# Which engine issues which loads of the scan: merge operands by GpSimd, late weights and attention operands by SyncE

## The chip, the cores and the metric

The kernel runs on one core of a Trainium2 chip. The metric is the device time of one execution in microseconds (us), the median of several runs. The engines are TensorE (PE: matmuls; PEld is its weight load), VectorE (DVE), ScalarE (ACT), GpSimd (POOL) and SyncE (SP), which does nothing but issue transfers (DMAs). Each engine works through its own list of instructions in order. Here DMAs are issued from SP, from ACT and from GpSimd; whichever engine issues one, it waits in its list until what the DMA needs is ready, and what stands behind it in that list waits with it.

## What the kernel computes

One layer of a transformer-like trunk on x of 1024 tokens by 1024 channels, in f32:

```python
mod = silu(c) @ W_ada + b_ada                 # shift, scale and gate, twice
h   = rmsnorm(x) * (1 + scale1) + shift1
proj = h @ w_in                               # q,k,v | delta-net q,k,v,z,beta,decay | branch gates
A = block_attention(rope(q), rope(k), v)      # 8 query heads, 2 kv heads, dim 64
# gated DeltaNet: 8 heads, 16 chunks of 64 tokens, forward and backward
def step(state, inp):
    u_n, w_n, a_n, qg_n, kd_n, gl_n = inp
    v_new = u_n - w_n @ state
    o_n = qg_n @ state + a_n @ v_new
    state = state * gl_n[..., None, None] + jnp.einsum('bhck,bhcv->bhkv', kd_n, v_new)
    return state, o_n
merged = sigmoid(gA) * (A @ W_attn_up) + sigmoid(gB) * (B @ W_dn_up)
x += gate1 * (merged @ W_o)
# then rmsnorm, modulation and a 16-expert SwiGLU MoE in which each expert picks its 128 tokens
```

The scan over chunks is serial: each step needs the state of the one before. `T` in the reference (the inverse of a 64 by 64 lower triangular matrix per chunk and head) is made in the kernel from its two diagonal 32 by 32 blocks' inverses and a merge that fills the block off the diagonal.

## The kernel before, in words

The layer runs as one program of stages: norms and first projections (to about 226 us), the chunk matrices (`dn_tile`, to about 300), their inverses with more projections beside them (to about 364), the **scan** (369 to 716), attention (to about 950), the merge of both branches (to about 1110), and the MoE to the end. The change lies in the scan.

The scan has 16 steps t; step t handles chunk t forward and chunk 15 - t backward. What a step does on PE, by line:

- L654: products of the state with k and q (32 matmuls of 64x64).
- L669: the inverse matrix W times the right side (16). VectorE makes that right side from L654's result (L658, L661).
- L684 and L691: state update and output (16 each; VectorE's L674, L675 ahead of them, L687 and L693 behind them).
- L630 and L637, the **merge** of the chunk matrices for the step after: 16 matmuls of 32x32 each, with ScalarE's L632 and L639 behind them.

Its small matmuls wait for VectorE, so fillers lie between them: the **late projections** (L1209), 14 column groups of 128 of `w_in`, each 48 matmuls of 128x128 by 512 (wh times hTh, wh times hTl, wl times hTh), 672 in all, taken from a generator by `fill(n)` with the counts `FILL = 8, 9, 9, 9, 60` and `END = 6, 6, 6, 6`: 35 in a step, 60 ahead of the first. Each group's weights come with `raw_load` (512 KB, tile wraw with two buffers) one group ahead, and ScalarE (L290, wh) and VectorE (L291, wl) split them into a high and a low part. Also beside the scan run the preparation of attention in steps 0 to 7 (transposes L149, norms and rotary, L744 to L809, whose results are stored to qT_d, kT_d and vS_d), the output of the scan from step 8 on (`scan_post`, L703 to L722), and the late modulation vectors (`mods_late`: loads L919, VectorE's L930 and L932).

A step's operands come through DRAM. `scan_load(t + 2)` issues, at step t, four loads of W (L610), two of the negated inverse blocks n_d (L612, tile name Sc) and two of wt_d (L613): 32 KB each, in runs of 128 bytes, for the **merge**; and further two each of kqs, kv and sa (L618 to L620) for the step itself. n_d and wt_d have one buffer with rows for even and odd chunks, W has two. `attn_load` issues, after step 8, the first operands of attention: two tiles kT (L816, L820), two qT (L818) and vS (L819), together about 3.5 MB.

The program is written for all engines at once; a list scheduler with cost estimates of its own then fixes the order of the instructions on each engine, across stages. So the code's order of `fill` calls isn't the order in which PE runs them, and a change of the issuing engine can change the order on the other engines too.

Of the kernel before, what the change touches and what calls it, by code (L numbers as in the profile page):

```python
# [7 lines left out]
F = mybir.dt.float32  # L8
# [77 lines left out]
class K:  # L86
# [194 lines left out]

    def raw_load(self, col):
        raw = self.wp.tile([128, 8, 128], F, name="wraw", bufs=2)
        self.nc.gpsimd.dma_start(raw, self.i["w_in"][0, :, col:col + 128].rearrange("(k p) c -> p k c", p=128))
        return raw

    def raw_split(self, raw):
# [310 lines left out]
    def scan_load(self, t):  # L598


        nc = self.nc
        w = self.W[t % 2]
        nf, at, kv = self.nf, self.sa[:, t % 2], self.kv[t % 2]
        quads, ns = [], (t, 15 - t)
        kq = [self.kqs[d][:, t % 2] for d in range(2)]
        for d, n in enumerate(ns):
            x = n % 2
            src = self.w_d[d].rearrange("(n h) (b s c) -> n b s h c", h=8, b=2, s=32)
            for b in range(2):
                nc.sync.dma_start(w[64 * x + 32 * b:64 * x + 32 * b + 32, :, b * 32:b * 32 + 32], src[n, b])  # L610
            f, o = slice(64 * x + 32 * d, 64 * x + 32 * d + 32), slice(64 * x + 32 - 32 * d, 64 * x + 64 - 32 * d)
            nc.sync.dma_start(nf[f], self.n_d[d, n].rearrange("h s c -> s h c"))  # L612
            nc.sync.dma_start(self.wt[f], self.wt_d[d].rearrange("(n h) (c s) -> n c h s", h=8, s=32)[n])  # L613
            quads.append((f, o, slice(32 * d, 32 * d + 32), slice(32 - 32 * d, 64 - 32 * d)))
        yield w, at, kv, kq, nf, quads
        for d, n in enumerate(ns):
            r = slice(64 * (n % 2), 64 * (n % 2) + 64)
            nc.sync.dma_start(kq[d], self.kq_d[n])  # L618
            nc.sync.dma_start(kv[r], self.kv_d[n // 2, r])
            nc.sync.dma_start(at[r].rearrange("p h c -> p (h c)"), self.a_d[d, n // 2, r])  # L620
        yield
# [188 lines left out]
    def attn_load(self, bp):  # L810
        nc = self.nc
        self.kT = [bp.tile([128, 2, S], R, name=f"kT{a}") for a in range(2)]
        self.qTs = [bp.tile([128, 512], R, name=f"qT{n}") for n in range(2)]
        self.vS = bp.tile([128, NT, 2, 128], R, name="vS")
        self.rv = self.misc.tile([128, 8, NT], F, name="rv")
        nc.gpsimd.dma_start(self.kT[0].bitcast(F), self.kT_d[0:2].rearrange("h p t -> p h t"))  # L816
        for n in range(2):
            nc.gpsimd.dma_start(self.qTs[n].bitcast(F), self.qT_d[0, :, n * 512:(n + 1) * 512])  # L818
        nc.gpsimd.dma_start(self.vS.bitcast(F), self.vS_d.rearrange("j p (a c) -> p j a c", a=2))  # L819
        nc.gpsimd.dma_start(self.kT[1].bitcast(F), self.kT_d[2:4].rearrange("h p t -> p h t"))  # L820

    def attn_setup(self):
        self.aP = [self.unit(g, (128, 2, 512), R, name="aP") for g in ("g17", "g18", "g12")]
# [863 lines left out]
```

## Time before, and how to read the profile

| | |
|---|---|
| median of three runs | 1728.37 us (1728.33 to 1729.34) |
| the profiled execution | 1728.42 us |
| its span in the trace | 1726.6 us |
| mean granted TensorE clock | 0.967 |
| PE busy | 1616.8 us (94%) |
| DVE busy | 1409.3 us (82%) |
| ACT busy | 907.1 us (53%) |
| POOL busy | 204.3 us (12%) |
| DMA packets, volume | 284146, 388.81 MB |

The profiled execution took 0.05 us more than the median, and 1.8 us lie outside its span. "Clock" or PEclk is the share of full TensorE speed that was granted (1.00 is 2.4 GHz, 0.5 is 1.2 GHz). A window row gives the stretch and its length, then for PE, PEld, DVE, ACT and POOL in this order the busy time and the number of instructions (only PE and PEld where one line alone is asked for), then the mean clock, the share of the 16 DMA engines' time that packets took, and GB/s. A timeline row gives the start, the length, the line and the number of matmuls put together, and in brackets the idle time before it and what ended that.

### The profile page before, as it was taken

The page shows a single profiled execution, that of the slowest core. Times are in us where ns is not written, and L with a number is a line of the kernel's source. Part 1 is how long each engine was busy: PE and PEld are TensorE (multiplying, and loading weights), DVE is VectorE, ACT ScalarE, POOL GpSimd, SP SyncE. Part 2 cuts the span into 40 slices and gives each one's busy share as a digit, 9 for nine tenths or more (in the row PEclk, how much of TensorE's full clock was granted, in tenths as well). Part 3 has the DMA queues.
Part 4 walks back from the last instruction along what each step waited for, and adds up shares of the span by engine and source line. Part 5 has one row for each costly group of instructions (what it writes and reads, how often), then busy time and mean ns, then how long its engine had stood idle before and what let it go on. Part 6 is the DMA issues. An engine that isn't in the chain of part 4 may idle for free. (4 is left out here: it accounts for less than half of the span.)

```text
span 1726.6 us, 30147 instructions
## 1 busy us (share of the span) xinstructions
PE 1616.8 (94%) x11131; PEld 1278.1 (74%) x11131; DVE 1409.3 (82%) x2470; ACT 907.1 (53%) x1352; POOL 204.3 (12%) x196
## 2 busy tenths in 40 slices
PE   6999999889999899699999999669999999999997
PEld 4777778677777677478887788557777777777786
DVE  6899897954667757789986567979999999999996
ACT  6654432122344213288871323347777777777775
POOL 0000022010100100021112312300011000110000
PEclk9999999998999999699999999879999999999999
DMA  9454377257778966721135464769999999999981
GB/s 280 129 175 131 104 181 195 82 179 171 184 197 225 273 176 182 196 86 38 38 111 182 155 209 147 259 227 351 384 379 374 382 388 383 375 377 384 385 309 25
DMA packets 284146, 388.81 MB, mean 225 GB/s; under 512 B 88219, under 2 KB 152399, under 8 KB 283487
## 3 DMA queue, kind: packets, MB, share of 16 engines
q1 hardware_dynamic: 263279, 325.54, 57.4%
q0 software_dynamic: 14096, 48.77, 10.3%
q10 hardware_dynamic: 6624, 12.59, 2.0%
q8 instruction: 88, 1.44, 0.4%
q14 instruction: 59, 0.48, 0.1%
HBM read 328.04 MB, written 58.77 MB: 224 GB/s over the span
## 5 line engine op out<-in xcount | busy, mean ns | idle before, releaser
L1576 DVE TENSOR_TENSOR ew<-er,ew 128x1024 fp32r<-128x1024 f32 x384 | 452.2, 1219 | 29.8 <-ACT ew L1575 29.7
L1575 ACT CAST ew<-er 128x1024 fp32r<-128x1024 f32 x384 | 391.0, 1049 | 137.9 <-PE pj L1629 105.4
L1629 PE MATMUL pj<-ew,xT 128*128 128x512 f32 x1536 | 367.6, 396 | 4.5 <-DVE ew L1576 4.5
L1629 PEld LDWEIGHTS pj<-ew,xT 128*128 128x128 f32 x1536 | 283.2, 188 | 76.2 <-DVE ew L1576 19.5
L1646 PE MATMUL tr<-ew,aT 128*128 128x512 f32 x768 | 191.3, 398 | 0.0
L1646 PEld LDWEIGHTS tr<-ew,aT 128*128 128x128 f32 x768 | 139.7, 188 | 30.4 <-DVE ew L1576 3.4
L297 PE MATMUL pj<-hTh,wl 128*128 128x512 f32 (+1 forms) x384 | 123.4, 399 | 6.5 <-DVE wl L279 6.5
L297 PE MATMUL pj<-hTh,wh 128*128 128x512 f32 (+1 forms) x384 | 122.0, 397 | 3.3 <-ACT hTh L258 1.8
L297 PE MATMUL pj<-hTl,wh 128*128 128x512 f32 (+1 forms) x384 | 121.5, 397 | 1.4 <-DVE hTl L261 1.4
L297 PEld LDWEIGHTS pj<-hTh,wl 128*128 128x128 f32 (+1 forms) x384 | 71.9, 188 | 23.7 <-DVE wl L279 6.9
L297 PEld LDWEIGHTS pj<-hTh,wh 128*128 128x128 f32 (+1 forms) x384 | 70.7, 187 | 20.6 <-ACT hTh L258 1.9
L866 DVE TENSOR_REDUCE am<-pj 128x1 f32<-128x1024 f32 x64 | 77.7, 1216 | 10.0 <-PE pj L861 9.5
L1652 POOL DMA_INDIRECT out_dram<-xe,idxT x16 | 37.2, 2327 | 407.9 <-DVE tok L1550 353.4
L297 PEld LDWEIGHTS pj<-hTl,wh 128*128 128x128 f32 (+1 forms) x384 | 71.2, 187 | 18.6 <-DVE hTl L261 2.0
L1255 PE MATMUL pj<-hTh,uw 128*128 128x512 f32 x256 | 83.5, 404 | 1.0 <-DVE uth L1261 0.5
L868 ACT ACTIVATE ap<-pj,am 128x1024 f32<-128x1024 f32 x64 | 71.8, 1123 | 20.7 <-DVE am L866 11.1
L1209 PE MATMUL pj<-hTh,wh 128*128 128x512 f32 x224 | 79.9, 423 | 0.8 <-ACT y L1214 0.8
L1209 PE MATMUL pj<-hTh,wl 128*128 128x512 f32 x224 | 79.4, 422 | 0.0
L1209 PE MATMUL pj<-hTl,wh 128*128 128x512 f32 x224 | 77.8, 416 | 0.0
L861 PE MATMUL pj<-kT,qT 128*128 128x512 f32 x256 | 76.3, 406 | 0.0
L278 ACT CAST wh<-wraw 128x1024 fp32r<-128x1024 f32 (+1 forms) x26 | 26.7, 1028 | 87.9 <-PE pj L297 87.9
L325 DVE SCALAR_TENSOR_TENSOR y<-xc,colt,y 128x1024 f32<-128x1024 f32 x48 | 61.4, 1279 | 1.4 <-ACT y L323 0.9
(391 smaller groups left out, 2899.0 us busy)
## 6 DMA issues: line engine op xcount, KB each, us to landing
er<-in_w_gate_dram SPq DMA_DIRECT2D x128, 512.0 KB
er<-in_w_up_dram SPq DMA_DIRECT2D x128, 512.0 KB
er<-in_w_down_dram SPq DMA_DIRECT2D x128, 512.0 KB
wraw<-in_w_in_dram POOLq DMA_DIRECT2D x36, 512.0 KB, 5.9
mw<-in_w_ada_dram SPq DMA_DIRECT2D x44, 256.0 KB
wt<-in_w_ada_dram SPq DMA_DIRECT2D x16, 512.0 KB
gate_d<-y ACTq DMA_DIRECT2D x32, 256.0 KB
kqs<-kq_d SPq DMA_DIRECT2D x32, 256.0 KB
```

The lines of the kernel that those rows point to most:

```text
L297: self.nc.tensor.matmul(ps[q][:n], w[:, k, :n], x[k][:, q * 512:(q + 1) * 512], start=(k == 0 and w is wh and x is self.hTh), stop=(k == 7 ...
L325: nc.vector.scalar_tensor_tensor(y, xc[:, t:t + S], w(t), y, op0=OP.mult, op1=OP.add)
L861: nc.tensor.matmul(ps[:, kh], qT[:, i * 128:(i + 1) * 128], self.kT[a][:, s, kh * 512:(kh + 1) * 512], start=(s == 0), stop=(s == 1), skip ...
L866: nc.vector.reduce_max(m, ps, axis=AX.X, negate=True)
L868: nc.scalar.activation(p, ps, AF.Exp, bias=m, scale=1.0, accum_out=self.rv[:, h, half * 4 + i:half * 4 + i + 1])
L1209: nc.tensor.matmul(ps[q], a[:, k], x[k][:, q * 512:(q + 1) * 512], start=(k == 0 and a is wh and x is self.hTh), stop=(k == 7 and a is wl))
L1255: nc.tensor.matmul(ps, w[:, k], v[k][:, qs], start=(k == 0 and p == 0), stop=(k == 3 and p == 2))
L1575: nc.scalar.copy(hi, raw)
L1576: nc.vector.tensor_sub(lo, raw, hi.bitcast(F))
L1629: nc.tensor.matmul(pg[m], x[:, 2 * kp + k], wi[:, k], start=(kp == 0 and k == 0 and n == 0), stop=(kp == 3 and k == 1 and n == 2))
L1646: nc.tensor.matmul(py[q], x[:, k], wi[:, q], start=(k == 0 and n == 0), stop=(k == 7 and n == 2))
L1652: nc.gpsimd.indirect_dma_start(out=out2, out_offset=bass.IndirectOffsetOnAxis(ap=self.idx[:, e:e + 1], axis=0), in_=y, in_offset=None, com ...
```

## The change

The engine that issues two kinds of loads is exchanged. The eight merge loads of each step (L610, L612, L613: 128 in all) go from SyncE to GpSimd. The 13 `raw_load` calls (L284) and the five loads of `attn_load` go from GpSimd to SyncE. No byte, buffer or matmul is added or taken away.

```diff
--- before.py
+++ after.py
@@ -281,7 +281,7 @@
 
     def raw_load(self, col):
         raw = self.wp.tile([128, 8, 128], F, name="wraw", bufs=2)
-        self.nc.gpsimd.dma_start(raw, self.i["w_in"][0, :, col:col + 128].rearrange("(k p) c -> p k c", p=128))
+        self.nc.sync.dma_start(raw, self.i["w_in"][0, :, col:col + 128].rearrange("(k p) c -> p k c", p=128))
         return raw
 
     def raw_split(self, raw):
@@ -607,10 +607,10 @@
             x = n % 2
             src = self.w_d[d].rearrange("(n h) (b s c) -> n b s h c", h=8, b=2, s=32)
             for b in range(2):
-                nc.sync.dma_start(w[64 * x + 32 * b:64 * x + 32 * b + 32, :, b * 32:b * 32 + 32], src[n, b])
+                nc.gpsimd.dma_start(w[64 * x + 32 * b:64 * x + 32 * b + 32, :, b * 32:b * 32 + 32], src[n, b])
             f, o = slice(64 * x + 32 * d, 64 * x + 32 * d + 32), slice(64 * x + 32 - 32 * d, 64 * x + 64 - 32 * d)
-            nc.sync.dma_start(nf[f], self.n_d[d, n].rearrange("h s c -> s h c"))
-            nc.sync.dma_start(self.wt[f], self.wt_d[d].rearrange("(n h) (c s) -> n c h s", h=8, s=32)[n])
+            nc.gpsimd.dma_start(nf[f], self.n_d[d, n].rearrange("h s c -> s h c"))
+            nc.gpsimd.dma_start(self.wt[f], self.wt_d[d].rearrange("(n h) (c s) -> n c h s", h=8, s=32)[n])
             quads.append((f, o, slice(32 * d, 32 * d + 32), slice(32 - 32 * d, 64 - 32 * d)))
         yield w, at, kv, kq, nf, quads
         for d, n in enumerate(ns):
@@ -813,11 +813,11 @@
         self.qTs = [bp.tile([128, 512], R, name=f"qT{n}") for n in range(2)]
         self.vS = bp.tile([128, NT, 2, 128], R, name="vS")
         self.rv = self.misc.tile([128, 8, NT], F, name="rv")
-        nc.gpsimd.dma_start(self.kT[0].bitcast(F), self.kT_d[0:2].rearrange("h p t -> p h t"))
+        nc.sync.dma_start(self.kT[0].bitcast(F), self.kT_d[0:2].rearrange("h p t -> p h t"))
         for n in range(2):
-            nc.gpsimd.dma_start(self.qTs[n].bitcast(F), self.qT_d[0, :, n * 512:(n + 1) * 512])
-        nc.gpsimd.dma_start(self.vS.bitcast(F), self.vS_d.rearrange("j p (a c) -> p j a c", a=2))
-        nc.gpsimd.dma_start(self.kT[1].bitcast(F), self.kT_d[2:4].rearrange("h p t -> p h t"))
+            nc.sync.dma_start(self.qTs[n].bitcast(F), self.qT_d[0, :, n * 512:(n + 1) * 512])
+        nc.sync.dma_start(self.vS.bitcast(F), self.vS_d.rearrange("j p (a c) -> p j a c", a=2))
+        nc.sync.dma_start(self.kT[1].bitcast(F), self.kT_d[2:4].rearrange("h p t -> p h t"))
 
     def attn_setup(self):
         self.aP = [self.unit(g, (128, 2, 512), R, name="aP") for g in ("g17", "g18", "g12")]
```

The scheduler's order moves with it. First GpSimd at the start of the scan: L581 clears the tile W, L284 are loads of late weights, L750 are two products of the rotary table. Before:

```order
L581 MEMSET W 128x1024
L284 DMA wraw<-in_w_in_dram 128x8x128 x2
L750 ISA
L750 TENSOR_TENSOR tab<-rp,rw 128x128 x2
L284 DMA wraw<-in_w_in_dram 128x8x128 x2
L750 TENSOR_TENSOR tab<-rp,rw 128x128 x2
L284 DMA wraw<-in_w_in_dram 128x8x128
L750 TENSOR_TENSOR tab<-rp,rw 128x128 x2
L284 DMA wraw<-in_w_in_dram 128x8x128
```

and with the change:

```order
L581 MEMSET W 128x1024
L612 DMA Sc<-n_d 32x8x32
L610 DMA W<-w_d 32x8x32 x2
L613 DMA Sc<-wt_d 32x8x32
L610 DMA W<-w_d 32x8x32 x2
L612 DMA Sc<-n_d 32x8x32
L613 DMA Sc<-wt_d 32x8x32
L610 DMA W<-w_d 32x8x32 x2
L612 DMA Sc<-n_d 32x8x32
```

GpSimd's list now holds the merge loads in the order of the steps, with nothing else between those of the first steps; its whole list for the scan is these 128 loads and the 16 products L750.

Second, SyncE's list about step 9, where attention's operands stand (L919 are loads of modulation weights, L722 the scan's output going to DRAM, L809 stores of attention's prepared q and k). Before:

```order
L610 DMA W<-w_d 32x8x32
L722 DMA dn_d<-dz 128x4x64 x2
L610 DMA W<-w_d 32x8x32
L612 DMA Sc<-n_d 32x8x32
L613 DMA Sc<-wt_d 32x8x32
L610 DMA W<-w_d 32x8x32 x2
L612 DMA Sc<-n_d 32x8x32
L613 DMA Sc<-wt_d 32x8x32
L919 DMA st<-in_w_ada_dram 128x512
L618 DMA kqs<-kq_d 128x512
```

and with the change:

```order
L809 DMA kT_d<-qst 128x4x128
L816 DMA kT_6104<-kT_d 128x2x1024
L722 DMA dn_d<-dz 128x4x64 x2
L818 DMA qT_6106<-qT_d 128x512
L818 DMA qT_6107<-qT_d 128x512
L819 DMA vS<-vS_d 128x8x256
L820 DMA kT_6105<-kT_d 128x2x1024
L618 DMA kqs<-kq_d 128x512
L619 DMA kv<-kv_d 64x1024
L620 DMA sa<-a_d 64x512
```

The merge loads are gone from SyncE's list, and the five loads of `attn_load` (L816 to L820) stand in it, right ahead of the kqs, kv and sa loads of a later step; the 13 loads of L284 stand at other places of the same list, two of them ahead of the first kqs load.

Third, PE in the last two steps of the scan (L861 are score matmuls of attention, L945 a product of the modulation vectors, L149 transposes). Before:

```order
L861 MATMUL pj<-kT_6104,qT_6107 128x512 x8
L669 MATMUL dn<-st,W 64x64 x16
L684 MATMUL dn<-st,kv 64x64 x8
L691 MATMUL dn<-st,sa 64x64 x16
L630 MATMUL tr<-Sc 32x32 x16
L684 MATMUL tr<-st,kv 64x64 x8
L654 MATMUL dn<-Sc,kqs 64x64
L637 MATMUL tr<-W,pt 32x32 x16
L654 MATMUL dn<-Sc,kqs 64x64 x31
L945 MATMUL tr<-macc,ones 1x512
L669 MATMUL dn<-st,W 64x64 x13
```

and with the change, in the last step:

```order
L669 MATMUL dn<-st,W 64x64 x16
L1209 MATMUL pj<-hTl_571,wh 128x512 x2
L1209 MATMUL pj<-hTh_570,wl 128x512 x2
L1209 MATMUL pj<-hTh_611,wh 128x512 x2
L691 MATMUL dn<-st,sa 64x64 x16
L1209 MATMUL pj<-hTl_612,wh 128x512 x2
L1209 MATMUL pj<-hTh_611,wl 128x512 x2
L1209 MATMUL pj<-hTh_652,wh 128x512 x2
```

Before, all 672 fillers stand ahead of the first of these rows: they have run out in step 13, no L1209 stands between the matmuls of the last two steps, and those steps have eight score matmuls. In the middle of the scan from 35 to 46 fillers stand between one step and the next. With the change 35 stand in every step, as a rule 18 of them ahead of L654, 8 between L654 and L669 and 9 between L669 and L684; L630 stands right ahead of L669, and L637 behind L691. Some 64 fillers are left behind the last step, with the first 16 score matmuls among them (32 stood ahead of the end of the scan before). On VectorE 16 of the 40 instructions of L930 and L932 now stand in steps 2 to 6; before, all 40 stood from step 8 on.

## Rows read from the trace of the kernel before

**Rows 1.** The page's part 2: the span in 40 slices of 43 us.

```profile
PE   6999999889999899699999999669999999999997
PEclk9999999998999999699999999879999999999999
```

**Rows 2.** Windows: stretches inside the scan, all engines.

```profile
382.20:401.15 18.95, 13.38 (x148) 9.15 (x146) 1.07 (x2) 2.07 (x5) 1.75 (x3) 0.64 0.89 176
401.15:554.00 152.85, 148.93 (x2229) 115.90 (x2225) 105.14 (x281) 60.30 (x135) 12.43 (x21) 1.00 0.73 194
685.00:715.80 30.80, 19.40 (x372) 14.87 (x370) 25.16 (x52) 6.85 (x13) 0.00 (x0) 0.72 0.67 172
369.00:715.80 346.80, 316.48 (x4441) 241.48 (x4440) 225.02 (x548) 104.60 (x218) 20.30 (x32) 0.94 0.76 201
```

**Rows 3.** Windows, the filler line L1209 alone.

```profile
382.20:401.15 18.95, 9.33 (x20) 5.27 (x18) 0.64 0.89 176
369.00:715.80 346.80, 189.91 (x672) 124.35 (x672) 0.94 0.76 201
499.79:517.18 17.39, 10.17 (x35) 6.18 (x35) 1.00 0.68 174
617.99:641.48 23.49, 17.18 (x66) 11.58 (x65) 1.00 0.67 171
```

**Rows 4.** Windows: two whole periods of the scan, all engines.

```profile
499.79:517.18 17.39, 17.31 (x258) 13.06 (x250) 11.22 (x32) 6.24 (x15) 0.88 (x2) 1.00 0.68 174
617.99:641.48 23.49, 23.49 (x292) 17.19 (x292) 15.67 (x34) 6.38 (x11) 0.00 (x0) 1.00 0.67 171
```

**Rows 5.** Timeline of PE: start, length, line, count, idle before.

```profile
387.12 0.28 PE L630 MATMUL tr<-Sc 32*32 32x32 f32 x2 [4.32 <-DMA Sc<-wt_d]
...
428.07 0.62 PE L1209 MATMUL pj<-hTh,wh 128*128 128x512 f32 x2
...
435.33 0.62 PE L1209 MATMUL pj<-hTl,wh 128*128 128x512 f32 x2
...
448.09 0.63 PE L149 MATMUL tr<-masks,hl 128*128 128x128 f32 x4 [0.95 <-DVE hl L795]
...
605.90 0.28 PE L630 MATMUL tr<-Sc 32*32 32x32 f32 x2 [7.45 <-DMA Sc<-wt_d]
...
606.71 1.05 PE L1209 MATMUL pj<-hTh,wh 128*128 128x512 f32 x2
...
611.83 0.57 PE L1209 MATMUL pj<-hTh,wh 128*128 128x512 f32 x1
```

**Rows 6.** Waits from 366 to 720: total, times, longest.

```profile
PE tr L630 <- DMA Sc<-wt_d: 14.5, 4, 7.5
```

**Rows 7.** Waits of SP's DMA queue, 366 to 720.

```profile
SPq L768 <- DVE vst L767: 38.6, 8, 14.4
```

**Rows 8.** Timeline of SP's queue, 585 to 606.

```profile
591.01 0.93 SPq L722 DMA_DIRECT2D dn_d<-dz  x2
...
592.53 4.40 SPq L612 DMA_DIRECT2D Sc<-n_d  x1
```

**Rows 9.** Groups of GpSimd (POOL) instructions, 200 to 720.

```profile
L525 POOL DMA_DIRECT2D n_d<-nn x32 | 18.6, 584 | 42.6 <-DVE nn L518 40.0 <-DVE e L510 2.3 <-issue 0.3
L284 POOL DMA_DIRECT2D wraw<-in_w_in_dram x13 | 11.7, 897 | 181.4 <-DVE wl L291 81.3 <-DVE ro_a L121 28.1 <-DVE wl L279 21.5
```

**Rows 10.** Source view of L284: issue to landing.

```profile
DMA to landing us min/median/max: 4.4/6.7/8.2
```

**Rows 11.** Source view of L525: issue to landing.

```profile
DMA to landing us min/median/max: 1.9/2.9/5.7
```

**Rows 12.** Source view of L612 on SP: one issue, ns.

```profile
L612 SPq DMA_DIRECT2D Sc<-n_d x32: 302/428/4399, 378.4 to 695.4; - x32
```

**Rows 13.** Groups of VectorE (DVE) instructions, 369 to 716.

```profile
L658 DVE TENSOR_TENSOR st<-dn,egs 128x256 f32<-128x256 f32 x64 | 24.3, 417 | 27.8 <-PE dn L654 27.7
L930 DVE SCALAR_TENSOR_TENSOR macc<-mw,cs,macc 128x512 f32<-128x512 f32 x14 | 10.4, 744 | 0.7 <-DMA mw<-in_w_ada_dram 0.7
```

## The prediction, made before the changed kernel ran

> **What bounds the kernel now.** The page comes first: PE has a 9 in most slices of 43 us; within the scan (slices 9 to 17) the busy digit falls to 8 in slices 9 and 14 and to 6 in 17, and the clock's to 8 in 10 and to 6 in 17 [rows 1]. Slices hide what is shorter, so the scan was then cut into windows. In its middle, from 401 to 554, PE is busy 148.93 of 152.85 us at clock 1.00, 97.4%: there PE itself is the limit, and DVE with 105.14 us isn't. The whole scan, 369 to 715.8, has PE busy 316.48 of 346.80 us at a mean clock of 0.94 [rows 2]. So the scan loses time in a few places, not everywhere. The timeline and the waits of PE tell which:
>
> 1. The start, 382.2 to 401.15: clock 0.64, PE busy 13.38 of 18.95 us [rows 2]. The first merge stands still for 4.32 us for wt [rows 5].
> 2. Step 11's merge at 598: PE stands 7.45 us for wt, and the 13 fillers after it run at half speed [rows 5]. All waits of PE for wt are 14.5 us in four [rows 6]. SyncE was late: its L722 store went out only at 591.0, L612 behind it took 4.40 us to issue [rows 8], against a median of 0.43 [rows 12].
> 3. The end, 685 to 715.8: no fillers are left (PE's order above), 372 small matmuls keep PE busy only 19.40 of 30.80 us at clock 0.72 [rows 2], each waiting for DVE, which is busy 25.16 there.
>
> **What is lost there, worked out.** A filler at full clock costs (435.33 - 428.07) / 32 = 0.227 us [rows 5]. A small matmul costs, from one period without idle time (17.39 us, 258 matmuls, 35 of them fillers [rows 3, 4]), (17.39 - 35 x 0.227) / 223 = 0.042 us.
>
> - Start: 20 fillers [rows 3] and 128 others are 4.5 + 5.4 = 9.9 us of work in 18.95: 9.0 lost.
> - Step 11: 7.45 of idling, and 14 fillers at 0.43 instead of 0.227 (606.12 to 612.33 is 13 of them after 606.71 [rows 5]): 3.0. Together 10.5.
> - End: 364 x 0.042 + 8 scores x 0.227 = 17.1 us of work in 30.8: 13.7 lost.
>
> Sum 33.2 us. A check by another way: the scan's busy time at its mean clock is 316.48 x 0.94 = 297.5 us of full-speed work; at the middle's 97.4% that takes 305.4, so 41.4 of the 346.8 us could go. With no idle time at all it would be 49.3, the most that can be won here. I take the middle of the two ways, 37.
>
> **The change part by part.**
>
> *Merge loads off SyncE.* 128 issues at a median of 0.428 us [rows 12] are 55 us of SyncE's list. None of it is on PE's path by itself; what counts is that a merge load no longer stands behind L722 or L768, whose waits on SyncE run to 14.4 us [rows 7]. This is what removes place 2's wait and most of place 1's.
>
> *Merge loads on GpSimd.* The trace of before has no such load there. The nearest rows are n_d's stores, the same 32x8x32 shape from the same engine: 584 ns each [rows 9], landing after 2.9 us, at most 5.7 [rows 11]; the upper bound is L284's 897 ns [rows 9] and its 8.2 us [rows 10]. Eight a step are 4.7 us (up to 7.2) of a 17.4 us period, with about 0.9 us of rotary products: GpSimd isn't full either way. I take 584, the same shape. A set is wanted two steps after its buffers come free, some 35 us, so 5.7 or 8.2 us of landing is covered. If that cover goes, the price is the landing time, per step: 16 x 2.9 = 46 us; I see nothing that takes it away, since GpSimd's list holds nothing else that waits.
>
> *The order on PE.* This is the bigger half. With every step holding 35 fillers, the last two steps aren't bare any more (place 3), and the 64 fillers and 16 scores behind the last step hide its sums. The fillers don't cost anything new: 672 stay 672 [rows 3]. Steps 11 to 13 had up to 66 fillers in one period (23.49 us [rows 3, 4]); by the same unit costs that period with 35 is 23.49 - 31 x 0.227 = 16.5 us. The 16 scores that move behind the scan cost the attention what they cost here: nothing net.
>
> *Late weights and attention operands on SyncE.* 18 issues, 13 of 512 KB. They cost SyncE some 18 x 0.43 = 8 us, far under the 55 it gives up. What they do is wait: L284 waits until VectorE has split an earlier group (GpSimd waited 81.3 us for it, which cost nothing there [rows 9]). On SyncE kqs, kv, sa, attention's stores and the L919 loads stand behind. kqs, kv and sa are double-buffered and issued a step ahead, 17 us; a wait of a few us is covered, one like L768's 14.4 [rows 7] isn't quite.
>
> *VectorE.* 16 L930 and L932 in steps 2 to 6 are 16 x 0.744 = 11.9 us [rows 13], 2.4 a step on top of 105.14 / 152.85 x 17.4 = 12.0: 14.4 of 17.4. And the new order leaves less between L654 and L669: 8 fillers and 16 L630 are 1.8 + 0.7 = 2.5 us, while VectorE needs three L658 (1.25 [rows 13]) and one subtraction of twice their size, about 0.8 as an estimate, 2.1 in all. If it is later than that by 0.4 us, PE waits. Such just-in-time waits are there now too, 0.95 us for hl [rows 5]. I charge 1 us in each of five full steps, 5 us; between 0 and 15 (every step) are the bounds.
>
> **Sum.** 37 - 5 = 32 us off. The profiled execution, 1728.42 us, stands 0.05 from the median, so no correction: **1696 us**. A difference under 0.2% (3.5 us) is about what a measurement here can't tell from none.
>
> **Rivals.**
>
> *Just-in-time waits in every step.* For it: the spacing 18, 8, 9 is tight, and DVE's list is long. Against: the middle of the scan runs at 97.4% with DVE at 69% [rows 2]. About 15 steps x 1 us instead of 5: 1706, with lower clock after the waits up to 1711; I put it at 1708.
>
> *The burst stalls again, on another load.* attention's 3.5 MB now stand in SyncE's own list right ahead of kqs, kv and sa. For it: beside that burst an issue took 4.40 us [rows 8]. Against: kqs has a step of lead. If PE stands as long as it did in step 11, 10.5 us come back: 1707.
>
> *The transfers were hidden anyway.* Only the four waits for wt, 14.5 us [rows 6], go, and the end of the scan stays as long because VectorE bounds it (25.16 of 30.80 us [rows 2]): 1714. The Trainium skill, "DMA: Bandwidth & Descriptors", section "Issuing engines are not separate DMA queues", says that DMAs of all engines end on the same 16 DMA engines, and that issuing from several saves only the sequencer's time, usually small; by that rule alone SyncE's 55 us, off PE's path, would bring nothing. Here the trace speaks against it: the stall of step 11 went with an issue of 4.40 us and the wait ahead of it, which are the sequencer's [rows 8].
>
> *No change.* What is won in the scan is waited for in attention, whose first operands arrive no sooner; the page shows clock and busy digits at 9 right behind the scan [rows 1], so this is unlikely: 1728.
>
> *Slower: late weights.* L284 stands in SyncE's list behind stores that wait, L768 for up to 14.4 us [rows 7], and lands 6.7 us after its issue [rows 10]. A group's matmuls can't start without it, and the small matmuls of the scan stand behind them in PE's list. Eleven groups load inside the scan, so each us of lateness costs up to 11; it decides from (32 + 3.5) / 11 = 3.2 us late each. With the landing wholly exposed, 11 x 6.7 = 74 - 32: 1770. Against: a load has one whole group, 48 fillers or some 24 us, of lead.
>
> **How the numbers follow.** My forecast, with its own range 1686 to 1703: 0.54. Waits in every step: 0.14. The burst again: 0.13. Hidden anyway: 0.06. No change: 0.05. Slower: 0.08. The range reaches up over the three partial cases to 1716 and down to what is left if the second way holds nearly whole (41 of 49 us without the charge for VectorE, and some of place 1's start earlier): 1678. What lies outside is no change, slower, and a few in a hundred below. Faster is the first four, 0.87; same 0.05; slower 0.08.
>
> **What would show it.** In the changed kernel's trace: L630 and L637 wait for no DMA (place 1 and 2 right); the clock is 1.00 from about 390 to the end of the scan; periods of 16.5 to 18 us in all 16 steps; a scan that ends some 32 us sooner, with the same length behind it. Wrong would be: waits of L669 or L684 for VectorE of over 1 us in most steps (first rival); a wait of L654 for kqs at about step 11 (second); the last steps as long as before (third); L1209 waiting for wl or wh, and SyncE's list waiting before L284 (the slower one). Steps 2 to 6 are where I expect the worst periods.

## The result, and the profile after

The changed kernel takes 1708.97 us (median of 4 runs, 1706.11 to 1711.86) against 1728.72 us in the runs of before beside it (1728.33 to 1729.34). The ratio is 0.9885, with a 95% interval of 0.9867 to 0.9904: 19.8 us faster, 1.15%. The forecast was 1696, 32 us. The time lies in the range of 1678 to 1716, but outside the forecast's own 1686 to 1703; the profiled execution, 1710.1 us, has a span of 1708.3.

First the page, its slices now 42.7 us long; rows of before are [rows 1]:

```profile
PE   5999999897979989999999999579999999999997
PEclk9999999998989999999999999789999999999999
```

The notch at the end of the scan, a 6 in both lines in slice 17, is gone: 16 and 17 have a 9. Now slices 10 and 12 have a 7 for PE and an 8 for the clock. The windows say the same (columns as in [rows 2]):

```profile
382.20:401.15 18.95, 9.93 (x144) 8.10 (x145) 3.89 (x9) 3.67 (x10) 2.52 (x5) 0.69 0.96 188
401.15:554.00 152.85, 137.64 (x2290) 110.94 (x2293) 118.47 (x310) 60.25 (x134) 56.50 (x89) 0.94 0.91 241
685.00:715.80 30.80, 28.38 (x134) 20.73 (x132) 16.69 (x20) 18.33 (x33) 8.83 (x7) 1.00 0.53 168
369.00:715.80 346.80, 307.36 (x4494) 240.41 (x4492) 239.50 (x578) 112.66 (x235) 96.04 (x150) 0.93 0.82 219
```

The end, 685 to 715.8, went from 19.40 us of PE time at clock 0.72 to 28.38 at 1.00. The start, 382.20 to 401.15, won nothing: 9.93 us of PE time now, 13.38 before [rows 2]. And the middle, which had been PE's own limit with 148.93 us busy at 1.00, is down to 137.64 at 0.94. So the change took out the bare end, left the start, and opened new places in the middle.

The last L691 of the scan starts at 679.1 instead of 714.0, but 64 fillers and all score matmuls lie behind it now; the first L1255 of the merge stage starts at 873.5 instead of 891.7, 18.2 earlier, and from there on all is shifted by 18 to 19 us. The whole difference arises in the scan and in the first us of attention.

Step by step the new middle looks like this. Each row is one period, from the start of L654 to the next one's, steps 1 to 7:

```profile
413.00:432.60 19.60, 17.04 (x280) 13.90 (x279) 14.67 (x38) 7.63 (x19) 8.16 (x12) 0.91 0.97 236
432.60:450.25 17.65, 16.16 (x278) 12.95 (x277) 12.77 (x33) 7.08 (x17) 4.62 (x8) 1.00 1.04 290
450.25:469.00 18.75, 16.23 (x278) 12.99 (x277) 12.77 (x37) 7.62 (x17) 6.02 (x10) 1.00 0.83 222
469.00:491.40 22.40, 18.07 (x278) 14.61 (x277) 19.48 (x51) 7.43 (x17) 8.68 (x11) 0.85 0.88 222
491.40:514.20 22.80, 18.58 (x278) 14.96 (x277) 18.02 (x43) 9.09 (x21) 7.89 (x12) 0.85 0.89 248
514.20:530.00 15.80, 15.70 (x278) 12.81 (x277) 13.21 (x36) 7.39 (x16) 6.03 (x10) 1.00 1.03 288
530.00:545.70 15.70, 15.70 (x278) 12.81 (x277) 13.48 (x36) 7.62 (x18) 4.63 (x8) 1.00 0.77 197
```

The last two rows are a step with nothing in its way: PE is busy 15.70 of 15.80 and of 15.70 us, with the same 278 matmuls. The prediction's unit costs gave 16.5 to 17.4. Of the 15.7 us the 243 matmuls that aren't fillers take 15.7 - 35 x 0.227 = 7.8; before, in the period from 460.48 to 479.64, PE was busy 18.77 us with 287 matmuls, 43 of them fillers, so that the 244 others took 18.77 - 43 x 0.227 = 9.0. The new order has them in longer runs, with fewer changes between small and large matmuls; that this is why was not tested. The five rows ahead of the last two are 2 to 7 us longer, 22.7 us in sum, and DVE is busy up to 19.48 of 22.40 us there. Behind step 7 two more periods are long, those of steps 10 and 13:

```profile
577.70:596.84 19.14, 16.48 (x261) 12.84 (x260) 13.57 (x31) 4.14 (x8) 4.61 (x8) 0.82 0.95 232
628.76:650.35 21.59, 17.56 (x267) 12.61 (x266) 16.88 (x44) 4.24 (x8) 2.30 (x4) 0.84 0.72 192
```

What PE waits for, at the start and in step 4, by its timeline:

```profile
385.27 0.66 PE L630 MATMUL tr<-Sc 32*32 32x32 f32 x30 [3.10 <-DMA Sc<-wt_d]
...
392.45 1.69 PE L654 MATMUL dn<-Sc,kqs 64*64 64x64 f32 x62 [2.58 <-DMA kqs<-kq_d]
...
397.50 1.51 PE L149 MATMUL tr<-masks,qraw 128*128 128x128 f32 x6 [3.37 <-DMA qraw<-qkv_d]
...
476.56 1.09 PE L149 MATMUL tr<-masks,hl 128*128 128x128 f32 x4 [4.33 <-DVE hl L795]
```

The start waits for wt, then kqs, then qraw; step 4 waits 4.33 us for hl, VectorE's last product of the preparation. That wait costs more than itself: the period is 22.40 us instead of 15.70, PE is busy 18.07 us of it for the 15.70 us of work, and the clock from 476.5 to 482.5 is 0.57. Of the other long periods step 1 waits 2.56 us for qraw, a DMA, step 10 stands 2.54 us at L669 for nothing that the profile names, and step 13 waits 4.03 us for the scan's own output on VectorE (L714), which makes PE's largest sum of waits from 366 to 720:

```profile
PE tr L149 <- DVE st L714: 9.0, 6, 4.0
```

VectorE in turn waits for the loads of the modulation work. Its largest wait from 405 to 520:

```profile
DVE macc L930 <- DMA mw<-in_w_ada_dram: 7.2, 3, 3.1
```

With the other tiles of these loads (mb, st and L932's mw) that is 13.4 us. The merge itself is out of the way: PE's waits for wt, 14.5 us in four before [rows 6], are one of 3.1, at the start, where GpSimd's load itself stands 3.6 us until the stage before has stored wt_d. GpSimd's groups from 360 to 700:

```profile
L610 POOL DMA_DIRECT2D W<-w_d x64 | 36.9, 583 | 32.4 <-PE dn L669 27.9 <-DMA w_d<-wb 3.2 <-issue 1.2
L612 POOL DMA_DIRECT2D Sc<-n_d x32 | 18.8, 588 | 95.6 <-PE tr L630 88.7 <-PE dn L669 4.5 <-DMA Sc<-n_d 2.3
L613 POOL DMA_DIRECT2D Sc<-wt_d x32 | 18.6, 582 | 7.0 <-DMA wt_d<-wtmp 3.6 <-DMA Sc<-wt_d 3.1 <-issue 0.2
```

and the source view of L612:

```profile
DMA to landing us min/median/max: 2.3/5.3/10.5
```

128 issues at 582 to 588 ns, where the prediction took 584 from n_d's stores [rows 9]. GpSimd spends its time waiting for PE to free the buffers (88.7 us before L612), so the loads go out as early as they can, some two steps ahead. They land after a median of 5.3 us, at most 10.5, more than the 2.9 and 5.7 taken from the stores [rows 11], and behind the start it doesn't matter, since they have two steps.

### The profile page after: what moved, and what is told of

It reads as the page before. It is cut to its first block, busy times and chain, and to the rows that moved or that the text cites. A ratio compares the mean times of both kernels' runs of the same rounds, so it can differ in the third digit from the quotient of the medians.

```text
span 1708.3 us, 30169 instructions
## 1 busy us (share of the span) xinstructions
PE 1593.8 (93%) x11131; PEld 1267.3 (74%) x11131; DVE 1409.8 (83%) x2470; ACT 906.1 (53%) x1352; POOL 274.8 (16%) x306
## 3 DMA queue, kind: packets, MB, share of 16 engines
q10 hardware_dynamic: 6624, 12.59, 2.0%
## 5 line engine op out<-in xcount | busy, mean ns | idle before, releaser
L866 DVE TENSOR_REDUCE am<-pj 128x1 f32<-128x1024 f32 x64 | 77.9, 1217 | 19.5 <-PE pj L861 19.0
L1255 PE MATMUL pj<-hTh,uw 128*128 128x512 f32 x256 | 83.4, 403 | 1.0 <-DVE uth L1261 0.5
L1209 PE MATMUL pj<-hTh,wh 128*128 128x512 f32 x224 | 77.6, 423 | 0.0
L1209 PE MATMUL pj<-hTh,wl 128*128 128x512 f32 x224 | 77.5, 418 | 0.0
L861 PE MATMUL pj<-kT,qT 128*128 128x512 f32 x256 | 74.7, 403 | 2.2 <-ACT ap L868 1.9
L1209 PE MATMUL pj<-hTl,wh 128*128 128x512 f32 x224 | 75.5, 413 | 0.0
```

What stands on the lines that cost most here:

```text
L861: nc.tensor.matmul(ps[:, kh], qT[:, i * 128:(i + 1) * 128], self.kT[a][:, s, kh * 512:(kh + 1) * 512], start=(s == 0), stop=(s == 1), skip ...
L866: nc.vector.reduce_max(m, ps, axis=AX.X, negate=True)
L1209: nc.tensor.matmul(ps[q], a[:, k], x[k][:, q * 512:(q + 1) * 512], start=(k == 0 and a is wh and x is self.hTh), stop=(k == 7 and a is wl))
L1255: nc.tensor.matmul(ps, w[:, k], v[k][:, qs], start=(k == 0 and p == 0), stop=(k == 3 and p == 2))
```

## The experiments

Theory 1: the gain is the even spread of fillers plus merge loads that no longer stand behind SyncE's waits; what is missing is PE waiting for VectorE in steps 1 to 5. Theory 2: late weights have to leave GpSimd for the merge loads to have a free list. Theory 3: what is missing is the transfer engines at the start and a half clock behind any wait. Each run is compared with the kernel before on the same chip (medians 1729.0 to 1730.6 there).

**Halves of the change.** The first run moves the merge loads alone.

```diff
-                nc.sync.dma_start(w[64 * x + 32 * b:64 * x + 32 * b + 32, :, b * 32:b * 32 + 32], src[n, b])
+                nc.gpsimd.dma_start(w[64 * x + 32 * b:64 * x + 32 * b + 32, :, b * 32:b * 32 + 32], src[n, b])
...
-            nc.sync.dma_start(nf[f], self.n_d[d, n].rearrange("h s c -> s h c"))
+            nc.gpsimd.dma_start(nf[f], self.n_d[d, n].rearrange("h s c -> s h c"))
...
```

> Half of the change alone: the 128 merge loads on GpSimd, the late weights and attention's operands stay on GpSimd as before, so all stand in one list. The order on PE is that of the changed kernel (35 fillers in every step). Theory 1 (the gain comes from the even spread of fillers and from merge loads that are no longer behind SyncE's stores; the missing part is PE waiting for VectorE): about 1709 us, within 1704 to 1714. Theory 2 (the late weights have to leave GpSimd, because a merge load behind an L284 that waits for VectorE stalls PE): waits of L630 for DMA come back, 1716 to 1730.

1706.6 us, ratio 0.9879 (0.9854 to 0.9904): the whole gain. Theory 2 falls. The second run moves the other half alone, L284 and `attn_load` to SyncE:

```diff
-        self.nc.gpsimd.dma_start(raw, self.i["w_in"][0, :, col:col + 128].rearrange("(k p) c -> p k c", p=128))
+        self.nc.sync.dma_start(raw, self.i["w_in"][0, :, col:col + 128].rearrange("(k p) c -> p k c", p=128))
...
-        nc.gpsimd.dma_start(self.kT[0].bitcast(F), self.kT_d[0:2].rearrange("h p t -> p h t"))
+        nc.sync.dma_start(self.kT[0].bitcast(F), self.kT_d[0:2].rearrange("h p t -> p h t"))
...
```

> The other half alone: late weights and attention's operands on SyncE, merge loads on SyncE as before, so GpSimd has neither. Here fillers reach to the last step too (39, 34, 35, 38, 23, 40 and so on, 551 ahead of the last L654, before 612 of 612). Theory 1, if the spread of fillers is the larger part: the bare end goes, some 14 us, the waits for wt stay: 1712 to 1718. Rival (the gain is the merge loads' own queue): nothing is won and SyncE's list is longer by 18 loads: 1728 or above.

1760.0 us, ratio 1.0184 (1.0157 to 1.0212): 31 us slower, against theory 1, and more than a list longer by 18 issues explains. This is the prediction's slower rival, late weights, come true in another kernel. SyncE's queue in this run:

```profile
587.20 0.38 SPq L816 DMA_DIRECT2D kT<-kT_d  x1
593.44 0.93 SPq L722 DMA_DIRECT2D dn_d<-dz  x2
594.42 1.00 SPq L818 DMA_DIRECT2D qT<-qT_d  x2
595.58 0.37 SPq L819 DMA_DIRECT2D vS<-vS_d  x1
596.00 0.58 SPq L820 DMA_DIRECT2D kT<-kT_d  x1
...
597.46 0.66 SPq L284 DMA_DIRECT2D wraw<-in_w_in_dram  x1
```

its timeline of PE:

```profile
610.05 1.22 PE L1209 MATMUL pj<-hTh,wh 128*128 128x512 f32 x2 [11.33 <-ACT wh L290]
```

and its waits from 366 to 760:

```profile
ACT wh L290 <- DMA wraw<-in_w_in_dram: 27.7, 7, 8.8
...
PE pj L1209 <- ACT wh L290: 23.7, 5, 11.3
```

SyncE issues kT, then stands till 593.44 for VectorE's dz; behind that come the rest of attention's operands and only then a raw load, at 597.46. ScalarE waits for it before it can make wh, and PE stands 11.33 us. In all ScalarE waits 27.7 us for wraw and PE 23.7 for wh; in the changed kernel ScalarE's wait is 3.8 us in one. So the second half does harm while SyncE's list is full, and none when the 128 merge loads are gone from it.

The third run of this group is the changed kernel with attention's five loads back on GpSimd (the last diff's lower part undone).

> The changed kernel with attention's five operand loads back on GpSimd: merge loads and those five on GpSimd, late weights on SyncE. If the burst of 3 MB in SyncE's list ahead of kqs, kv and sa costs something (a rival of the prediction), 3 to 8 us faster, 1701 to 1706; if not, 1707 to 1711.

1709.0 us, ratio 0.9897 (0.9874 to 0.992): no difference. Which engine issues that burst doesn't show in the time. It shows in the trace: on GpSimd merge loads behind the burst stand 4.1 and 3.7 us until its vS and kT have landed, and PE's stall at L669 in step 10 is 7.3 us instead of 2.5.

**Half of the merge loads.** The next two runs leave all else as it was before and move either L610 or L612 and L613. In both the order on PE is the even one.

```diff
-                nc.sync.dma_start(w[64 * x + 32 * b:64 * x + 32 * b + 32, :, b * 32:b * 32 + 32], src[n, b])
+                nc.gpsimd.dma_start(w[64 * x + 32 * b:64 * x + 32 * b + 32, :, b * 32:b * 32 + 32], src[n, b])
```

> Only the 64 loads of W (L610) go to GpSimd; the n_d and wt_d loads (L612, L613), for which PE waited before, stay on SyncE, as do all others where they were. The order on PE is the even one (35 fillers a step, 531 ahead of the last L654), and VectorE's modulation work stands from step 7 on. Theory 1a (the even order carries the gain): 1695 to 1706. Theory 1b (the wait for wt behind SyncE's list has to go): L630 still waits for DMA, 1712 to 1725.

```diff
-            nc.sync.dma_start(nf[f], self.n_d[d, n].rearrange("h s c -> s h c"))
-            nc.sync.dma_start(self.wt[f], self.wt_d[d].rearrange("(n h) (c s) -> n c h s", h=8, s=32)[n])
+            nc.gpsimd.dma_start(nf[f], self.n_d[d, n].rearrange("h s c -> s h c"))
+            nc.gpsimd.dma_start(self.wt[f], self.wt_d[d].rearrange("(n h) (c s) -> n c h s", h=8, s=32)[n])
```

> Only the 64 loads of n_d and wt_d (L612, L613) go to GpSimd, W stays on SyncE. The order on PE is the even one here too, modulation work from step 6 on. Theories 1a and 1b both: 1693 to 1705. If it needs all 128 off SyncE: 1712 to 1725, with waits of L637 for W.

1712.0 us, ratio 0.9905 (0.988 to 0.993), and 1715.1, ratio 0.9919 (0.9907 to 0.9932). The waits from 366 to 720 with W alone moved (its profiled execution, span 1721.0, was one of its longer ones):

```profile
PE tr L630 <- DMA Sc<-wt_d: 8.6, 2, 5.5
PE tr L149 <- DMA qraw<-qkv_d: 8.6, 5, 5.8
```

and with n_d and wt_d alone:

```profile
PE dn L669 <- issue: 14.8, 2, 11.0
PE dn L654 <- DMA kqs<-kq_d: 8.3, 2, 5.3
...
PE tr L149 <- DMA qraw<-qkv_d: 5.7, 4, 4.0
```

With wt left on SyncE PE still waits 8.6 us for it. With wt on GpSimd it waits 3.6 for wt, but kqs (8.3) and qraw are late, which have always been SyncE's, and not W, as was expected. PE also stands 14.8 us at L669 there for nothing that the profile names, the longer time (11.0) from 587.0 on, when SyncE had just taken 10.87 us to issue four loads of W (574.59 to 585.46); whether W is what it waits for isn't shown. Theory 1a, that the even order carries the gain, fails with both runs: it wanted 1706 or less. Theory 1b, that the wait for wt has to go, was too narrow: in these two runs wt, kqs and qraw, left in the longer SyncE list, are late. In both runs the modulation work stands from step 6 or 7 on, so they are to be compared with the next pair, not with the changed kernel.

**VectorE in steps 2 to 6.** The changed kernel with one tiny instruction, through which the late modulation work depends on step 7:

```diff
+                cs = self.misc.tile([128, 8], F, name="csl")
+                self.nc.vector.scalar_tensor_tensor(cs, self.X[:, 0, 0:8], 0.0, self.cs, op0=OP.mult, op1=OP.add)
+                self.cs = cs
                 behind.append(self.mods_late(MODG, 8))
```

> The changed kernel, with the late modulation work (L919 loads beyond the first four, L930, L932) made to depend on step 7 by a small VectorE instruction, so that it can't stand in steps 2 to 6. Theory 1 (VectorE's added work and its waits for L919 in steps 2 to 6 make PE wait for hl and the state): the long periods of 19 to 23 us shrink, 1701 to 1705. Theory 3 (the missing part is DMA contention at the start and the half clock behind any wait): 1707 to 1711, as the changed kernel.

1695.9 us, ratio 0.9806 (0.9781 to 0.9831): 13.1 below the run with attention's loads back, which is the changed kernel's time on that chip. The middle, in the same window as above:

```profile
401.15:554.00 152.85, 145.53 (x2479) 117.36 (x2477) 126.28 (x335) 63.43 (x140) 58.65 (x90) 0.97 0.94 253
```

and two of its periods, steps 4 and 5:

```profile
464.65:480.54 15.89, 15.89 (x278) 12.80 (x278) 13.37 (x37) 7.22 (x18) 6.04 (x10) 1.00 1.00 256
480.54:496.21 15.67, 15.67 (x279) 12.74 (x278) 13.37 (x36) 7.49 (x17) 6.96 (x10) 1.00 0.99 272
```

2479 matmuls instead of 2290 in the same 152.85 us, and steps 2 to 6 take 15.67 to 15.94 us, without a wait of VectorE for these loads: theory 1's cause, with more behind it than was expected of it. Step 1, with its wait for qraw, stays at 20.03 us, and the held work is paid for later in part: step 8 takes 21.57 us there. The same edit on the kernel that moves the merge loads alone:

> Merge loads on GpSimd, late weights and attention's operands left on GpSimd, and the late modulation work held to step 7 as in the earlier run of that kind. If the exchange of the late weights does nothing for the gain and the held work gives its 13 us here too: 1690 to 1700. If late weights in the merge loads' own list cost something once VectorE isn't the limit: 1702 to 1708.

1698.2 us, ratio 0.9816 (0.9803 to 0.9828). Both halves of the change together are worth no more than the first here either. Against these two the halves of the merge loads are 14 to 19 us slower: about as much as the even order with half of the loads had brought. So the even order alone isn't the gain; taking the rest of the merge loads off SyncE is worth as much again.

**Another list.** The merge loads on ScalarE's list, all else as before (`nc.scalar` for `nc.gpsimd` in the first diff):

> As the run with the merge loads alone moved, but to ScalarE's list in place of GpSimd's. The order on PE is the even one, modulation work stands in steps 1 to 4. If all that counts is that they leave SyncE's list: 1702 to 1712, as there. If the list they stand in has to be free of waiting work: a load behind a waiting L762 or L290 stands, and ScalarE's own work stands behind a load that waits, 1715 to 1740.

1717.3 us, ratio 0.9921 (0.9902 to 0.9941), in the second of the two ranges, at its lower end. Waits from 366 to 720, of ScalarE and of PE:

```profile
ACT qst L807 <- DMA W<-w_d: 19.0, 3, 7.7
PE tr L630 <- DMA Sc<-wt_d: 8.9, 3, 4.2
```

L807, a product of attention's preparation, needs no W, so it stood behind a load in ScalarE's list that waited. Leaving SyncE's list, with the even order, brings 13 us even so; the list of an engine with waiting work of its own costs some 7 (by the ratios) to 11 us (by the medians) of the 22 again. The two intervals touch, so the size is rough.

**The start and the burst.** On the held kernel the rotary weights' six small loads (L732, L736) go ahead of the inversion stage, their tile in another pool:

```diff
-        self.rw = self.misc.tile([128, 2, 2, 64], F, name="rw")
+        self.rw = self.ab.tile([128, 2, 2, 64], F, name="rw")
...
+            self.rope_weights()
             with ExitStack() as st2:
...
             self.scan_setup()
-            self.rope_weights()
```

> The changed kernel with the held modulation work, and the six small loads of the rotary weights (L732, L736) issued before the inversion stage, so that SyncE's list goes straight on to kqs, kv, sa and qraw at the start of the scan. If the start is lost because these stand behind nine us of issues: the waits for kqs and qraw (some 9 us in the profile) shrink, 1688 to 1693. If the transfer engines are full there whatever the order: 1693 to 1699, as with the hold alone.

1683.7 us, ratio 0.9734 (0.9721 to 0.9748): 12.2 below the held kernel, more than was expected. SyncE's queue at the start in the changed kernel:

```profile
367.94 0.33 SPq L732 DMA_DIRECT2D rw<-in_q_norm_w_dram  x1
368.33 4.76 SPq L736 DMA_DIRECT2D rw<-in_q_norm_w_dram  x2
...
377.08 0.41 SPq L618 DMA_DIRECT2D kqs<-kq_d  x1
```

the same in this run:

```profile
368.16 2.71 SPq L618 DMA_DIRECT2D kqs<-kq_d  x1
```

the stretch between, first in the changed kernel and then in this run:

```profile
377.00:382.20 5.20, 5.17 (x25) 3.93 (x23) 1.68 (x3) 1.54 (x2) 2.06 (x5) 1.00 0.33 87
377.00:382.20 5.20, 5.20 (x24) 4.32 (x23) 0.00 (x0) 0.68 (x1) 3.32 (x6) 1.00 1.08 282
```

and this run's window of the start:

```profile
382.20:401.15 18.95, 15.55 (x311) 12.31 (x310) 11.77 (x33) 5.29 (x14) 8.90 (x15) 1.00 1.09 250
```

In the changed kernel kqs goes out at 377.08, behind 9 us in which SyncE issues six loads of 16 and 32 KB; here at 368.16, and PE is busy 15.55 of the 18.95 us at clock 1.00 instead of 9.93 at 0.69. So the transfer engines (theory 3) weren't what bound the start: in the changed kernel their share is 0.33 from 377.0 to 382.2, while kqs has only just gone out, and here it is 1.08 there and 1.09 behind it. PE's first wait for wt shrinks too, from 3.78 us in the held kernel to 1.22, and step 1, which had waited for qraw, is down from 20.0 to 16.2 us.

Attention's five loads, spread over steps 8 to 11, each made to wait for its step by a tiny copy into its tile:

```diff
+        x = self.X[:, 0, 0:8]
+
+        def mark(t):
+            nc.vector.tensor_copy(t, x)
+
+        yield
+        mark(self.kT[0][:, 0, 0:8])
         nc.sync.dma_start(self.kT[0].bitcast(F), self.kT_d[0:2].rearrange("h p t -> p h t"))
+        yield
...
```

> The changed kernel with the held modulation work, and attention's five operand loads spread over steps 8 to 11, each behind a tiny VectorE copy that depends on its step. If the stall near step 10 (4.3 us inside L669 in the profile of the held run, and the half clock behind it) comes from the burst of 3 MB: 1689 to 1693. If it has another cause: 1694 to 1699.

1689.3 us, ratio 0.9778 (0.976 to 0.9795): 6.6 below the held kernel, but that one ran on another chip and the two intervals overlap, so this pair doesn't show a gain. And both:

> Both edits on the held kernel. If both places are worth what their waits show: 1682 to 1689. If neither: 1694 to 1699.

1676.4 us, ratio 0.9698 (0.9685 to 0.9711), 53 us below the kernel before and the fastest here, faster than was expected of both. On the same chip it is 7.3 us below the run with the early rotary weights alone and 12.9 below the one with the spread alone, with intervals apart: that is what each edit is worth on top of the other. Its page's part 2:

```profile
PE   6999999899998999999999999399999999999997
PEclk9999999999999999999999999699999999999999
```

and its windows of the start and the scan:

```profile
382.20:401.15 18.95, 17.77 (x342) 14.23 (x345) 13.43 (x37) 7.30 (x18) 7.39 (x14) 1.00 1.12 266
...
369.00:715.80 346.80, 327.94 (x4687) 258.88 (x4686) 269.28 (x623) 142.01 (x288) 96.67 (x150) 0.99 0.83 221
```

From slice 2 to 17 PE stands at 8 or 9, and the clock at 9 throughout the scan.

**The control:** all three edits on the kernel before, with no engine exchanged.

> The control: the kernel before, no engine exchanged, with all three edits of the fastest run (rotary weights early, attention's operands spread over steps 8 to 11, modulation work held to step 7, where it stood anyway). The order on PE is the uneven one, the last two steps bare. If these edits work without the exchange, the start and step 11 come out, 53 of the fastest run's us less some 15 for the bare end: 1690 to 1700. If the merge loads in SyncE's list and the bare end are what binds first: 1712 to 1728.

1722.4 us, ratio 0.9952 (0.9938 to 0.9965). 8 us, where they bring 33 on top of the exchange. Its window of the end:

```profile
685.00:715.80 30.80, 18.76 (x266) 12.45 (x261) 23.83 (x57) 6.32 (x12) 0.00 (x0) 0.62 0.79 211
```

PE's waits for wt are down from 14.5 to 1.3 us without any exchange, and kqs goes out at 380.29 instead of 385.88, still behind merge loads; the last L691 starts at 704.4 instead of 714.0. But the order stays uneven and the end as bare as before (19.40 us at 0.72 [rows 2]). So the waits for wt of places 1 and 2, taken away by themselves, are worth 8 us, where the prediction charged 19.5 for these places; at the start PE is then busy 14.25 us of the 18.95, at 0.91.

## Why the prediction was right in part

*The places.* Place 3, the bare end, was right: the window of the end went from 0.72 to 1.00. That the order is its cause, not the end's own work, is shown by the runs: in both with half of the loads moved, which have the even order, PE is busy 29.2 and 29.4 of its 30.8 us at 1.00; in the control, with the uneven order but hardly a wait for wt, 18.76 at 0.62. How much of the 19.8 us it carries isn't shown: no run has the even order with all merge loads on SyncE. Place 2, step 11's wait for wt, went as foreseen. Place 1, the start, 9.0 us of the sum, was not won at all, and this is a step that failed: it took the wait for wt [rows 5] behind SyncE's stores to be the cause, but on GpSimd PE still waited 3.1 us for wt, and then for kqs and qraw, which stood behind the rotary weights' issues in SyncE's list. The early rotary weights brought 12 to 13 us, part of them in step 1, so this term was about right in size and wrong in what would release it.

*GpSimd.* 584 ns an issue, taken from the stores, was 582 to 588; that two steps of lead cover the landing held, though the landing was twice what was taken.

*VectorE.* This is the term that was mis-sized: 5 us charged for steps 2 to 6, 13.1 measured by taking the cause away. The prediction had the place, the cause (16 more instructions there) and the bounds (0 to 15), and took the lower third. Two things were missing. VectorE waits in order for the L919 loads that come with that work, 13.4 us from 405 to 520; and behind a wait of some us PE ran at the lower clock (0.57 from 476.5 to 482.5), so that step 4's wait of 4.33 us made its period 6.7 us longer. The held run moves work and loads together, so how much of the 13 us is VectorE's time and how much its waits for L919 stays open.

*The sum.* 37 less 9 for the start and 13 for VectorE is 15; 19.8 were measured. What the working left out goes both ways, and no run closes the account. A clean step takes 15.7 us, not 16.5; and the first us of attention, where PE had stood for VectorE three times between 715.8 and 720 (0.97, 1.40 and 1.09 us), are now filled but for 0.60. Against that the periods of steps 10 and 13 are 3.4 and 5.9 us longer than a clean one. The check by another way took PE's busy time for work; the same small matmuls took 9.0 us of it in the old order and 7.8 in the new, so that the limit given, 49.3 us, wasn't one: the fastest run won 53. A small slip: 14 fillers at 0.43 instead of 0.227 us are 2.8 us, not 3.0.

*The rivals.* Just-in-time waits came nearest: 1706 to 1711 was given for them, 1709 measured, but by luck, since the waits are few and long and are those of L149 for hl and for the scan's output, not of L669 or L684 in most steps. The burst, spread out, gives 7.3 us, less than the 10.5 given; that was run with the burst on SyncE only. That the transfers were hidden anyway is refuted by the gain at the end and by the run with the merge loads alone: what counted is what 128 issues and their waits stand ahead of, and the order that came with moving them. The Trainium skill's rule ("DMA: Bandwidth & Descriptors", "Issuing engines are not separate DMA queues") is that another issuing engine saves only sequencer time, usually little. The 22 us of the run with the merge loads alone don't refute it, because the order on PE and VectorE changed along with the issuer. Late weights, the slower rival, didn't come in this kernel, and came with 31 us in the one where SyncE kept the merge loads: the mechanism was right, and it came only where the merge loads were still in that list.

*The marks.* L630 and L637 waiting for no DMA: nearly (one wait of 3.1 us). The clock at 1.00 from 390: wrong, 0.94. Periods of 16.5 to 18 us: 15.7 where nothing waits, up to 22.8 in steps 2 to 6, which were named as the worst, and 21.6 in step 13, which wasn't named.

## What to carry to other kernels

Put loads that a serial stage needs just in time in a list where little else waits, and ask what else stands there: GpSimd's list brought 22 us (and fewer packets, below), ScalarE's, with waiting work of its own, 13. The exchange's second half (moving other loads the other way) may be worth nothing, as here, or 31 us of loss if the first is missing. Under a scheduler with costs of its own, read the new order on all engines before costing a change of one queue: here an exchange of DMA engines spread the fillers evenly (a part of the gain) and pulled foreign work onto VectorE and the transfer engines (13 us of loss), and one tiny instruction that adds a dependence gave it back. When one wait is taken away, list what else arrives in the same us: at the start kqs and qraw stood right behind wt.

## What the runs showed of the hardware

*Packets.* The same 128 merge loads, 4.2 MB, are cut differently by the issuing engine. GpSimd's queue on the pages of the kernel before and of the run that moves the merge loads alone (packets, MB, share of the 16 engines' span):

```profile
q0 software_dynamic: 14096, 48.77, 10.3%
q0 software_dynamic: 18192, 52.97, 11.6%
```

That is 4096 packets more, 32 a load, while SyncE's queue loses 34816 (263279 to 228463), 272 a load; from ScalarE they are 34816 again (6624 to 41440). So GpSimd's list and fewer packets came together, and no run separates the two. The run on ScalarE's list wins 13 us with all the packets, so they aren't the whole gain. The share of the engines' time hardly differs: 1.3% of the span more on GpSimd's queue, 1.7% more on ScalarE's (2.0 to 3.7).

*Issues on SyncE* aren't of fixed length: 0.43 us in the median for L612 before [rows 12], but 4.76 us for two of L736 at the start, where the transfer engines' share is 0.98 (368 to 377), and 10.87 us for four of W beside attention's burst in the run with n_d and wt_d alone moved.

*GpSimd's small products* L750 became slower. The source view in the changed kernel (ns, least, median, most):

```profile
L750 POOL TENSOR_TENSOR tab<-rp,rw x16: 449/684/3043, 398.0 to 529.5; 128x128 f32<-128x128 f32 x16
```

In the kernel before they took 448 to 474 ns, 456 in the median, with the same shape. Loads in the same list aren't shown to be the cause: with the merge loads on ScalarE the median is 643, and with all 128 of them on GpSimd in the fastest run it is 463. Only the longest ones, over 2 us, are found just where GpSimd issues the loads of W. Nothing waited for L750 here.

*A stall of PE without a name.* PE stood at L669 in step 10 for nothing that the profile names ("issue"): 2.5 us in the changed kernel, 4.3 and 3.5 in the held one and the one with early rotary weights, each some 20 us behind the issue of attention's first load. Where the five loads are on GpSimd beside merge loads it was longer: 7.0 us with the merge loads alone moved, 6.8 with these and the modulation work held, 7.3 with the five loads put back, 11.0 with n_d and wt_d alone moved; with W alone moved it was 3.1 us, one step later. With the burst spread it was 1.6 and 1.2. What holds PE there stays open.
